# A hybrid decoder layer: z's blocks by sevens of products, and part of the state-space work on ScalarE

## The chip, the cores and the metric

The kernel runs on one core of one Trainium2 chip. The time is device microseconds of one execution. Three executions of the kernel before took 1457.78 to 1458.51 us, with a median of 1458.33. A separate execution was taken by the hardware profiler; it took 1458.42 us, of which its trace spans 1456.6. Engines are called by the profile's names: PE (TensorE), PEld (its weight loads), DVE (VectorE), ACT (ScalarE), POOL (GpSimd), SP (SyncE).

## What is computed

One layer for 256 tokens of width 2048, all in float32. The part that matters is the first half, `hybrid_mixer`, cut:

```python
u = rmsnorm(h)                                  # (256, 2048)
z, xbc, dt_raw, q, k, v = split(u @ w_in)       # z: 2048 columns; x: 2048, B and C: 1024 each; dt: 32; q, k, v: 2048 each
xs, bm, cm = split(silu(causal_depthwise_conv(xbc, conv_w, conv_b)))     # four taps
dt = softplus(dt_raw + dt_bias)                 # 32 heads in 8 groups of 4
a_cs = cumsum(dt * -exp(a_log))                 # inside chunks of 128 tokens
decay_in = exp(where(causal, a_cs[i] - a_cs[j], -inf))
y = (C B^T * decay_in) (x dt) + C state * exp(a_cs) + d_skip * x
y_ssm = groupnorm(y * silu(z)) * ssm_norm_w
y_att = dilated_window_attention(q, k, v)
h = h + rmsnorm(concat(y_ssm, y_att) @ w_out)
h = h + rmsnorm(relu(rmsnorm(h) @ w_up)^2 @ w_down)
```

## The kernel before

**Products in three parts.** A float32 operand is split in two: `hi` is its value rounded to PE's format (ACT, L147) and `lo` what is left (a subtraction on DVE, L148). A product is then three matmuls: hi by hi, hi by lo, lo by hi. Weights come in tiles of 256 rows by 512 columns, loaded by SP as `raw` (128 partitions x 1024), split into `hi` and `lo`, and used. One index `k` stands for 256 inputs, so eight of them make up the 2048. There are a few buffers for each, and PE's progress frees them.

**Plain work and sevens.** In plain work by tokens (`row_tile`, L328 to L330) two halves of the tokens, two halves of `k` and three matmuls make 12 matmuls of 128x512 for a block of 512 columns, so 24 for two blocks. A *seven* (`seven`, L411 to L413) takes two blocks at once and replaces the eight products of two token halves, two input halves and two blocks by seven products of sums (21 matmuls). Before it, sums of the activations are formed once for a `k` (`sums_of_acts`, L368 to L371 and a split), and for each seven sums of the weights (`add_in_line`, L252) that are split as well. `combine_new` (L420 to L424) puts the extra accumulators together. A `unit` runs a list of such `k` for two blocks, some plain and some by seven, and ends with plain ones. It takes all eight accumulator banks.

**Pairs.** For a seven, the sum of two weight tiles (a *pair*) comes from DRAM: POOL loads one tile to a place in DRAM (L276) and adds the other to it with a second, accumulating transfer (L277); SP loads the result later. `plan` lists the pairs in order, and `next_pair` issues the next. There are five places, and the first use of each is preceded by a tiny transfer (L275) that waits for a certain tile. In the kernel before, sevens are used from the second block of keys on, and the first four pairs are issued there.

**The state-space stage** (about the first 360 us). For each half: a block of B, one of C, then twice a block of x and one of z. B, C and x are computed with features on partitions (`gemm_features`, L473 and L476), put together (`added`, L496 and L497), scaled, and run through the convolution (`conv`: a padded copy on L736, the first tap on L741, three more on L743, and SiLU on L745). z is computed by tokens (`gate_block`, with SiLU on L751). In between, generators in a queue, `waiting`, are advanced a step at each `pump()`: `steps` (dt: a product on L660 and L661 with weights `raw_dt`, which ACT's queue loads on L653, then a chain of small DVE operations up to L693 and the cumulative sums on L698 to L706), and `ssd_group`, one for each of the eight groups (decay exponents on L790, their exponential on L791, the state products on L795 and after). `rstd` (1 / root mean square of each token) is made by POOL on L142.

**Order.** Each engine carries out its instructions in the order of its queue. A scheduler sets that order from the program's; work under `high_priority` goes ahead of other work.

**After the mixer**, `mix_to_up` adds the output product to h, normalizes it, and turns its rows by blocks of 128 (`turn`, L1108) to be the operand of the next product. `turn(t, n)` turns the four blocks of token half t and column block n.

Of the kernel before, what the change touches and what calls it, by code (L numbers as in the profile page):

```python
# [77 lines left out]
def hymba_layer(ctx: ExitStack, tc: tile.TileContext, x, norm_mix_pre, w_in, conv_w, conv_b, dt_bias, a_log,  # L78
# [177 lines left out]
    w_v, w_ups, w_downs = w_in[:, COL_V:], [w_up[:, hf * 4096:] for hf in range(2)], [w_down, w_down[4096:]]  # L256
# [10 lines left out]
    def next_pair():  # L267
# [6 lines left out]
        if len(paired) < len(places):  # L274
            nc.gpsimd.dma_start(d[:, 0:1], sh[:, NK - 1, 0:1].bitcast(F32))  # L275
# [149 lines left out]

    for n in (0, 2):
        plan("v", w_v, n, range(7), V_SEVENS)
# [223 lines left out]
    def steps():  # L651
# [16 lines left out]
        y = sp1.tile([P, NT, 32], F32, name="dt_y")  # L668
        for t in range(NT):
            nc.vector.scalar_tensor_tensor(y[:, t], p[:, t * 32:(t + 1) * 32], rstd[:, t:t + 1], bias_b,  # L670
                                           op0=ALU.mult, op1=ALU.add)

        e = sp1.tile([P, NT, 32], F32, name="dt_e")
        nc.vector.scalar_tensor_tensor(e, y, -1.0, y, op0=ALU.mult, op1=ALU.min)
        nc.scalar.activation(e, e, AF.Exp)
        r = sp1.tile([P, NT, 32], F32, name="dt_r")
        nc.vector.tensor_scalar(r, e, 2.0, None, op0=ALU.add)
        nc.vector.reciprocal(r, r)
        s = sp1.tile([P, NT, 32], F32, name="dt_s")
        nc.vector.tensor_mul(s, e, r)  # L680
        q = sp1.tile([P, NT, 32], F32, name="dt_q")
        nc.vector.tensor_mul(q, s, s)
        h = sp1.tile([P, NT, 32], F32, name="dt_h")
        nc.vector.tensor_scalar(h, q, 2.0 / 17, None, op0=ALU.mult)
        for n in (15, 13, 11, 9, 7, 5, 3):
            nc.vector.scalar_tensor_tensor(h, h, 2.0 / n, q, op0=ALU.add, op1=ALU.mult)
        nc.vector.scalar_tensor_tensor(h, h, 2.0, s, op0=ALU.add, op1=ALU.mult)
        nc.vector.scalar_tensor_tensor(dt, y, 0.0, h, op0=ALU.max, op1=ALU.add)
        ea = sp1.tile([P, 32], F32, name="dt_a")
        nc.scalar.activation(ea, a_b, AF.Exp)  # L690
# [41 lines left out]
    def conv(dst, ft0):  # L732
        for b in range(2):
# [4 lines left out]
            for f in range(2):  # L738
                ft = ft0 + 2 * b + f
                d = dst[:, 2 * b + f]  # L740
                nc.vector.tensor_scalar(d, pad[:, f, 3:], cw[:, 3, ft:ft + 1], None, op0=ALU.mult)  # L741
# [5 lines left out]
    def gate_block(c0):  # L747
        acc = gemm_tokens(w_in, c0, act_u, NK)
        dst = mp.tile([P, NT, NB], F32, name="tk", bufs=3)
        for t in range(NT):  # L750
            nc.scalar.activation(dst[:, t], acc[t], AF.Silu, scale=rstd[:, t:t + 1])  # L751
        return dst

    def ssd_group(sp, g, bT, cT, xT, z):
# [3 lines left out]
        nc.scalar.dma_start(bc, acs_d[hs].partition_broadcast(P))  # L758

# [9 lines left out]
        nc.vector.tensor_copy(bn, p[:, S:S + P])  # L769
# [16 lines left out]
        for c in range(NT):  # L786
            m = bc[:, :, c * P:(c + 1) * P]
            for r in range(HPG):
                h = HPG * g + r
                nc.vector.tensor_scalar(m[:, r], m[:, r], acs[:, c, h:h + 1], 0.0, op0=ALU.subtract, op1=ALU.min)  # L790
            nc.scalar.activation(m, m, AF.Exp)  # L791
            nc.vector.tensor_tensor(m, m, cbm[:, c, None, :].to_broadcast([P, HPG, P]), op=ALU.mult)
# [4 lines left out]
        nc.vector.tensor_copy(st, p[:, :S])  # L797
# [34 lines left out]
    sp = ssd.enter_context(tc.tile_pool(name="sp", bufs=2, side="right", reuse_waits="tile"))  # L832
    for hb in range(2):
# [644 lines left out]
```

## Time and profile before

| | |
|---|---|
| median of three runs | 1458.33 us (1457.78 to 1458.51) |
| profiled execution | 1458.42 us |
| its span | 1456.6 us |
| mean granted PE clock | 0.999 |
| instructions in the trace | 20308 |
| matmuls | 7117 |
| moved by DMA | 325.10 MB |

Rows of the trace give a start, a duration, the engine, the line, the operation with `out<-in`, sizes, a count, and in brackets how long the engine was idle before it and what released it. Rows of groups give count, busy time, mean ns of one, and the idle time before. A line number is one of the kernel before. Matmuls overlap on PE: one that lasts 0.39 us is followed by the next in less, so that starts are to be compared, not durations. ACTq is ACT's queue issuing a DMA.

### The profile page before, as it was taken

What the parts mean: (1) busy time and instruction counts of PE and PEld (TensorE: products, weight loads), DVE (VectorE), ACT (ScalarE), POOL (GpSimd) and SP (SyncE); (2) the same over time, 40 slices, a digit from 0 to 9 for tenths busy, and PEclk for the clock granted to TensorE, in tenths of its full rate; (3) what the DMA queues carried; (4) which work ended last, traced back from release to release, by engine and by line L of the source; (5) the groups of instructions that cost most, each with busy time, mean ns of one, the idle gap of its engine ahead of it and who ended that gap; (6) DMA issues with size and microseconds to landing.
All of it is one profiled execution on the core that took longest, in us unless ns stands there. A gap on an engine that the chain in (4) does not pass through costs nothing.

```text
span 1456.6 us, 20308 instructions
## 1 busy us (share of the span) xinstructions
PE 1448.5 (99%) x7117; PEld 1222.2 (84%) x7117; DVE 1268.3 (87%) x1886; ACT 897.8 (62%) x1227; POOL 146.2 (10%) x214
## 2 busy tenths in 40 slices
PE   9999999999999999999999999999999999999998
PEld 8888888888888888888888888888888888888886
DVE  6798897798987686689878999999889999999997
ACT  7465665465666556556557577666454776766663
POOL 0003100211110000001100111011111111101000
PEclk9999999999999999999999999999999999999999
DMA  8766666567875486688876798678888888798854
GB/s 270 209 205 179 184 179 197 178 175 231 237 224 174 130 235 209 191 255 270 260 226 216 205 313 242 193 227 253 241 248 279 251 245 245 210 293 263 250 176 159
DMA packets 168758, 325.10 MB, mean 223 GB/s; under 512 B 15328, under 2 KB 18256, under 8 KB 168656
## 3 DMA queue, kind: packets, MB, share of 16 engines
q1 hardware_dynamic: 144496, 272.37, 58.3%
q0 software_dynamic: 16288, 37.76, 13.2%
q10 hardware_dynamic: 7872, 13.68, 2.7%
q8 instruction: 56, 0.92, 0.2%
q14 instruction: 46, 0.38, 0.1%
HBM read 319.53 MB, written 41.98 MB: 248 GB/s over the span
## 4 chain that ended last, share of the span: by engine, by line
PE 99%; DVE 0%; ACT 0%; issue 0%; ACTq 0%
PE acc L473 15%; PE acc L328 12%; PE acc L330 12%; PE acc L329 12%; PE acc L476 8%; PE acc L413 6%; PE acc L411 6%; PE acc L412 6%; PE ps L330 3%; PE ps L329 3%; PE ps L328 3%; PE ps L413 2%; PE ps L411 2%; PE ps L412 2%; PE ps L807 1%; PE acc L1385 1%
## 5 line engine op out<-in xcount | busy, mean ns | idle before, releaser
L147 ACT ACTIVATE hi<-raw 128x1024 fp32r<-128x1024 f32 (+1 forms) x392 | 409.8, 1051 | 268.6 <-PE acc L473 92.2
L148 DVE TENSOR_TENSOR lo<-raw,hi 128x1024 fp32r<-128x1024 f32 (+1 forms) x392 | 476.9, 1221 | 92.7 <-ACT hi L147 88.7
L473 PE MATMUL acc<-ua,hi 128*128 128x512 f32 x600 | 163.5, 401 | 0.0
L473 PEld LDWEIGHTS acc<-ua,hi 128*128 128x128 f32 x600 | 105.7, 189 | 16.7
L147 ACT ACTIVATE hi<-e 128x1024 fp32r<-128x1024 f32 x64 | 68.0, 1063 | 71.4 <-DVE e L252 66.3
L328 PE MATMUL acc<-hi,ua 128*128 128x512 f32 x248 | 98.4, 397 | 0.0
L330 PE MATMUL acc<-hi,ua 128*128 128x512 f32 x248 | 96.8, 390 | 0.0
L476 PEld LDWEIGHTS acc<-ua,lo 128*128 128x128 f32 x600 | 88.2, 189 | 10.3
L329 PE MATMUL acc<-lo,ua 128*128 128x512 f32 x248 | 96.7, 390 | 0.0
L476 PE MATMUL acc<-ua,lo 128*128 128x256 f32 x600 | 90.8, 281 | 0.0
L328 PE MATMUL acc<-hi,sh 128*128 128x512 f32 x224 | 88.4, 395 | 0.0
L330 PE MATMUL acc<-hi,sl 128*128 128x512 f32 x224 | 87.3, 390 | 0.0
L329 PE MATMUL acc<-lo,sh 128*128 128x512 f32 x224 | 87.2, 389 | 0.0
L148 DVE TENSOR_TENSOR lo<-e,hi 128x1024 fp32r<-128x1024 f32 x64 | 77.9, 1218 | 0.0
L473 PE MATMUL acc<-uc,hi 128*128 128x512 f32 x240 | 68.5, 397 | 0.0
L411 PE MATMUL acc<-hi,ah 128*128 128x512 f32 x174 | 67.8, 389 | 0.0
L412 PE MATMUL acc<-lo,ah 128*128 128x512 f32 x174 | 67.7, 389 | 0.0
L413 PE MATMUL acc<-hi,al 128*128 128x512 f32 x174 | 67.7, 389 | 0.0
L148 DVE TENSOR_TENSOR lo<-ha,hi 128x1024 fp32r<-128x1024 f32 x43 | 52.4, 1220 | 6.0 <-ACT hi L147 5.7
L147 ACT ACTIVATE hi<-ha 128x1024 fp32r<-128x1024 f32 x43 | 45.3, 1057 | 18.3 <-PE acc L330 9.8
L330 PEld LDWEIGHTS acc<-hi,ua 128*128 128x128 f32 x248 | 46.6, 188 | 10.0
L328 PEld LDWEIGHTS acc<-hi,ua 128*128 128x128 f32 x248 | 46.6, 188 | 9.4 <-ACT ua L149 0.3
(543 smaller groups left out, 3510.9 us busy)
## 6 DMA issues: line engine op xcount, KB each, us to landing
raw<-in_w_in_dram SPq DMA_DIRECT2D x167, 512.0 KB, 3.9
raw<-in_w_down_dram SPq DMA_DIRECT2D x72, 512.0 KB, 5.2
raw<-in_w_up_dram SPq DMA_DIRECT2D x65, 512.0 KB, 4.6
raw<-in_w_out_dram SPq DMA_DIRECT2D x38, 512.0 KB, 5.0
pair<-in_w_up_dram POOLq DMA_DIRECT2D x56, 256.0 KB, 5.3
pair<-in_w_down_dram POOLq DMA_DIRECT2D x50, 256.0 KB, 6.3
raw<-pair SPq DMA_DIRECT2D x46, 256.0 KB, 4.6
ha<-in_w_up_dram SPq DMA_DIRECT2D x20, 512.0 KB, 5.7
```

Source lines behind the costliest of these rows:

```text
L147: return (nc.scalar.activation(hi, src, AF.Copy), nc.vector.tensor_tensor(lo, src, hi.bitcast(F32), op=ALU.subtract))
L148: nc.vector.tensor_tensor(lo, src, hi.bitcast(F32), op=ALU.subtract))
L328: nc.tensor.matmul(dst, a_h[:, r, ts], hi[:, j], start=begin and j == 0, stop=False)
L329: nc.tensor.matmul(dst, a_h[:, r, ts], lo[:, j], start=False, stop=False)
L330: product[t] = nc.tensor.matmul(dst, a_l[:, r, ts], hi[:, j], start=False, stop=end and j == KB - 1)
L411: nc.tensor.matmul(dst, a_h, hi[:, j], start=own and first, stop=False)
L412: nc.tensor.matmul(dst, a_h, lo[:, j], start=False, stop=False)
L413: nc.tensor.matmul(dst, a_l, hi[:, j], start=False, stop=own and last)
L473: nc.tensor.matmul(acc[f], hi[:, j, f * P:(f + 1) * P], u(k0 + j), start=k0 + j == 0, stop=False, skip_group_check=True)
L476: nc.tensor.matmul(acc[f][:, 0], lo[:, j, f * P:(f + 1) * P], u(k0 + j)[:, 0], start=False, stop=k0 + j == NK - 1, skip_group_check=True)
L807: nc.tensor.matmul(p[:, c, r], bc[:, r, c * P:(c + 1) * P], xdt[:, c, r], start=True, stop=True)
L1385: nc.tensor.transpose(p[:, f * P:(f + 1) * P], r[:, f * P:(f + 1) * P], ident)
```

## The change

1. **z by sevens.** The four calls of `gate_block` become two calls of `gates`, after the first and the third block of x. Each is a `unit` of two blocks, with `k` in the orders (0, 2, 4, 6, 1, 3, 5) and (0, 2, 1, 4, 3, 6, 5), sevens for 1, 3 and 5, and 7 plain at the end.
2. **Pairs from the start.** z's six pairs are listed ahead of the others. The first four are issued as soon as `u(15)`, the last tile of u, is there.
3. **Sums of activations** for k = 1, 3, 5 are made in the first stage, and once more for the keys.
4. **To ScalarE:** the first tap of the convolution, the exponents of decay (four activations Relu for each chunk of 128, with -1 as scale and the cumulative sum as bias, then the exponential with scale -1), and the copies `bn` and `st`.
5. **Order:** the dt chain goes ahead of other work and its products come some steps later in the count of steps; a group waits a step after its DMA; the first keys advance the queue two steps and one in turn instead of one; and in `mix_to_up` `turn(0, 2)` comes ahead of `turn(1, 0)`, with the banks set by a list.

```diff
-    w_v, w_ups, w_downs = w_in[:, COL_V:], ...
+    w_z, w_v, w_ups, w_downs = w_in[:, COL_Z:], w_in[:, COL_V:], ...
...
-            nc.gpsimd.dma_start(d[:, 0:1], sh[:, NK - 1, 0:1].bitcast(F32))
+            nc.gpsimd.dma_start(d[:, 0:1], u(NK - 1)[:, 0, 0:1].bitcast(F32))
...
+    plan("z", w_z, 0, (0, 2, 4, 6, 1, 3, 5), (1, 3, 5))
+    plan("z", w_z, 2, (0, 2, 1, 4, 3, 6, 5), (1, 3, 5))
...
         yield
-        for t in range(NT):
-            nc.vector.scalar_tensor_tensor(dA[:, t], dt[:, t], -1.0, ea, op0=ALU.mult, op1=ALU.mult)
-        yield
-        yield
+        with tc.high_priority(offset=AHEAD):
+            for t in range(NT):
+                nc.vector.scalar_tensor_tensor(dA[:, t], dt[:, t], -1.0, ea, op0=ALU.mult, op1=ALU.mult)
+        for _ in range(7):
+            yield
...
-                nc.vector.tensor_scalar(d, pad[:, f, 3:], cw[:, 3, ft:ft + 1], None, op0=ALU.mult)
+                nc.scalar.activation(d, pad[:, f, 3:], AF.Copy, scale=cw[:, 3, ft:ft + 1])
...
-    def gate_block(c0):
-        acc = gemm_tokens(w_in, c0, act_u, NK)
-        dst = mp.tile([P, NT, NB], F32, name="tk", bufs=3)
-        for t in range(NT):
-            nc.scalar.activation(dst[:, t], acc[t], AF.Silu, scale=rstd[:, t:t + 1])
-        return dst
+    def gates(n):
+
+        room["own"] = deque(mp.tile([P, NT, NB], F32, name="tk", bufs=3)[:, t] for t in range(NT))
+        place_of_sums()
+        room["sums"] = [v[:, k:k + KB] for k in range(NK // 2, NK, KB) for v in (sh, sl)]
+        room["raw"], room["turn"], room["acts"] = [], 0, act_u
+        gated = [mp.tile([P, NT, NB], F32, name="tk", bufs=3) for _ in range(2)]
+
+        def end(b):
+            def at_end(t, a):
+                with tc.high_priority(offset=AHEAD):
+                    v = gated[b][:, t]
+                    nc.vector.tensor_tensor(v, a, v, op=ALU.subtract if b else ALU.add)
+                    nc.scalar.activation(v, v, AF.Silu, scale=rstd[:, t:t + 1])
+            return at_end
+
+        unit(w_z, n, orders["z", n], (7,), *eight_banks(),
+             lambda x: combine_new([[v[:, t] for t in range(NT)] for v in gated], x), 0, (end(0), end(1)))
+        return gated
...
         nc.scalar.dma_start(bc, acs_d[hs].partition_broadcast(P))
+        yield
...
-        nc.vector.tensor_copy(bn, p[:, S:S + P])
+        nc.scalar.activation(bn, p[:, S:S + P], AF.Copy)
...
-                nc.vector.tensor_scalar(m[:, r], m[:, r], acs[:, c, h:h + 1], 0.0, op0=ALU.subtract, op1=ALU.min)
-            nc.scalar.activation(m, m, AF.Exp)
+                nc.scalar.activation(m[:, r], m[:, r], AF.Relu, scale=-1.0, bias=acs[:, c, h:h + 1])
+            nc.scalar.activation(m, m, AF.Exp, scale=-1.0)
...
-        nc.vector.tensor_copy(st, p[:, :S])
+        nc.scalar.activation(st, p[:, :S], AF.Copy)
...
+    with tc.high_priority(offset=AHEAD):
+        for _ in range(PAIRS_AHEAD):
+            next_pair()
+    zs = []
...
-            z = gate_block(COL_Z + xb * NB)
+            if xb % 2 == 0:
+                zs += gates(xb)
...
-    qk = [keys_too(0)]
+    qk = [keys_too(0, (2, 1))]
...
+    sums_of.clear()
...
-    with tc.high_priority(offset=AHEAD):
-        for _ in range(PAIRS_AHEAD):
-            next_pair()
...
-            turn(1, 0)
-            turn(0, 2)
+            turn(0, 2)
+            turn(1, 0)
```

Three queues show what this does to the order. The first is POOL's at the program's start; before, it held memsets of the convolution's edges (`pad`), then `rstd`, then more memsets:

```order
L735 MEMSET pad 128x2x3 x2
L142 ISA
L142 TENSOR_TENSOR rstd<-rm,half 128x2
L735 MEMSET pad 128x2x3 x6
L781 TENSOR_TENSOR xdd<-xdt,toend 128x256
```

After the change the five tiny transfers (L275) and then these rows stand there:

```order
L276 DMA pair_89<-in_w_in_dram 128x512
L276 DMA pair_90<-in_w_in_dram 128x512
L276 DMA pair_91<-in_w_in_dram 128x512
L276 DMA pair_92<-in_w_in_dram 128x512
L277 DMA pair_89<-in_w_in_dram 128x512
L277 DMA pair_90<-in_w_in_dram 128x512
L277 DMA pair_91<-in_w_in_dram 128x512
L277 DMA pair_92<-in_w_in_dram 128x512
L276 DMA pair_93<-in_w_in_dram 128x512
L739 MEMSET pad 128x2x3 x2
L142 ISA
L142 TENSOR_TENSOR rstd<-rm,half 128x2
```

So nine transfers of z's weights have moved ahead of the first memsets and of `rstd`.

The second is DVE's queue while PE works on the first z block. Before, subtractions for the weights (`lo`) alternate with the convolution of x (L736 to L743):

```order
L148 TENSOR_TENSOR lo<-raw,hi 128x1024
L743 SCALAR_TENSOR_TENSOR cT<-pad,cw,cT 128x256 x2
L736 TENSOR_TENSOR pad<-cT,rbc 128x2x256
L743 SCALAR_TENSOR_TENSOR cT<-pad,cw,cT 128x256
L741 TENSOR_SCALAR cT<-pad,cw 128x256 x2
L148 TENSOR_TENSOR lo<-raw,hi 128x1024
L743 SCALAR_TENSOR_TENSOR cT<-pad,cw,cT 128x256 x4
L148 TENSOR_TENSOR lo<-raw,hi 128x1024
```

After the change this is the second of the first unit's sevens (its first two additions stand just ahead) and the third:

```order
L148 TENSOR_TENSOR lo<-raw,hi 128x1024
L252 TENSOR_TENSOR tk<-cT,raw 128x512
L148 TENSOR_TENSOR lo<-cT,hi 128x1024
L148 TENSOR_TENSOR lo<-raw,hi 128x1024
L148 TENSOR_TENSOR lo<-tk,hi 128x512
L252 TENSOR_TENSOR cT<-raw 128x512
L252 TENSOR_TENSOR cT<-cT,raw 128x512
L148 TENSOR_TENSOR lo<-raw,hi 128x1024
L252 TENSOR_TENSOR tk<-cT,raw 128x512
L148 TENSOR_TENSOR lo<-cT,hi 128x1024
L148 TENSOR_TENSOR lo<-raw,hi 128x1024
L148 TENSOR_TENSOR lo<-tk,hi 128x512
```

Each seven now stands there as three additions of weights and four subtractions, without other work between the last two of them.

The third is ACT's queue where the first two groups' decays are made (`bc`). Before, this was behind the first z block, and ACT made only the exponentials (L791):

```order
L147 ACTIVATE hi<-raw 128x1024
L776 ACTIVATE xs<-ps 128x512
L791 ACTIVATE bc<-bc 128x4x128
L147 ACTIVATE hi<-raw 128x1024
L791 ACTIVATE bc<-bc 128x4x128 x2
L776 ACTIVATE xs<-ps 128x512
```

After the change the exponents (L816) and the exponentials (L817) stand among the splits of the first unit's sevens:

```order
L147 ACTIVATE hi<-raw 128x1024
L816 ACTIVATE bc<-bc,acs 128x128
L147 ACTIVATE hi<-tk 128x512
L147 ACTIVATE hi<-raw 128x1024
L816 ACTIVATE bc<-bc,acs 128x128 x3
L817 ACTIVATE bc<-bc 128x4x128
L816 ACTIVATE bc<-bc,acs 128x128 x4
L147 ACTIVATE hi<-cT 128x1024
L147 ACTIVATE hi<-raw 128x1024
L147 ACTIVATE hi<-tk 128x512
L420 ACTIVATE tk<-ps 128x512
```

So eight of the small activations and one exponential are now in the same queue between two splits of weights.

More of the change, by code (lines that the diff above doesn't have):

```diff
@@ L1066, in mix_to_up @@
         up = [bank() for _ in range(NT)]
[L1067 removed]
+        banks, turned = {}, {}
+        turns = [(0, 0), (0, 1), (1, 0), (0, 2), (1, 1), (1, 2), (1, 3), (0, 3)]
         weighed = hp.tile([P, NT, NB], F32, name="e")
```

67 lines of the change are left out of this document (34 added, 33 removed).

## Prediction, before the result was known

> **What bounds the kernel now.** I read the page's busy shares and its chain first, then the busy time by stretches of 40 us, then single stretches of the trace. The page says who sets the end:
>
> ```profile
> span 1456.6 us, 20308 instructions
> PE 1448.5 (99%) x7117; PEld 1222.2 (84%) x7117; DVE 1268.3 (87%) x1886; ACT 897.8 (62%) x1227; POOL 146.2 (10%) x214
> PE 99%; DVE 0%; ACT 0%; issue 0%; ACTq 0%
> ```
>
> The chain that ended last is TensorE almost from end to end. Whether that holds in the stages that the change touches (0 to 360 us) is in the stretches; the columns are the stretch, PE, weight load, DVE, ACT, POOL, clock, DMA share and GB/s:
>
> ```profile
> 0.00:40.00 40.00, 38.94 (x224) 34.70 (x225) 25.32 (x43) 27.06 (x55) 1.13 (x7) 1.00 0.83 267
> 40.00:80.00 40.00, 40.00 (x245) 35.68 (x244) 31.94 (x60) 22.18 (x29) 0.21 (x2) 1.00 0.67 201
> 80.00:120.00 40.00, 40.00 (x209) 33.84 (x208) 38.92 (x88) 27.46 (x39) 7.20 (x10) 1.00 0.64 197
> ...
> 280.00:320.00 40.00, 40.00 (x210) 34.04 (x209) 38.76 (x80) 28.40 (x41) 7.72 (x8) 1.00 0.63 182
> ...
> 360.00:400.00 40.00, 40.00 (x179) 33.16 (x178) 39.22 (x53) 23.85 (x28) 7.11 (x11) 1.00 0.90 246
> ```
>
> PE is busy all of the time, and DVE, at 38.92 of 40 where z0 stands, is close behind. So a product that PE need not do is time gained, and there is no idle PE time there to win besides. What counts is whether DVE, ACT and the DMAs still arrive first. Busy time hides overlap, so the price of a product is read from starts:
>
> ```profile
> 82.19 0.40 PE L328 MATMUL acc<-hi,ua 128*128 128x512 f32 x1
> 82.42 0.40 PE L329 MATMUL acc<-lo,ua 128*128 128x512 f32 x1
> ...
> 90.83 0.39 PE L330 MATMUL acc<-hi,ua 128*128 128x512 f32 x1
> ```
>
> From 82.19 to 90.83 there are 38 steps: (90.83 - 82.19) / 38 = 0.227 us a product, though one lasts 0.39.
>
> **The sum, against 1458.42 us** for the profiled execution (span 1456.6 and 1.8 around it); the median of the three runs is 1458.33, so the same differences are taken from the median.
>
> *Products.* Two units of two z blocks have three sevens each, and a seven has 21 products where plain work has 24: 6 x 3 = 18 fewer, 18 x 0.227 = **-4.1 us**. The small products between them stay the same in kind.
>
> *Transposes.* PE waits once here:
>
> ```profile
> 771.03 0.74 DVE L1099 SCALAR_TENSOR_TENSOR ha<-mw,rmix,ha 128x512 f32<-128x512 f32 x1
> 772.22 0.75 DVE L1099 SCALAR_TENSOR_TENSOR ha<-mw,rmix,ha 128x512 f32<-128x512 f32 x1
> 773.03 0.65 PE L1108 MATMUL acc<-ident,ha 128*128 128x128 f32 x4 [0.23 <-DVE ha L1099]
> ```
>
> `turn(1, 0)` needs the row of 772.22, ready at 772.97; `turn(0, 2)` needs the earlier one, of 771.77. With their order turned the wait of 0.23 goes, **-0.2** (0 to -0.4); what is late next is `turn(1, 0)`, which now comes one group of four transposes later, when its row is there.
>
> *DVE's and ACT's load.* The prices, as mean ns after the busy sum, by groups of equal shape:
>
> ```profile
> L148 DVE TENSOR_TENSOR lo<-raw,hi 128x1024 fp32r<-128x1024 f32 x113 | 141.1, 1250 | 32.1 <-ACT hi L147 30.9 <-PE acc L476 0.3
> L147 ACT ACTIVATE hi<-raw 128x1024 fp32r<-128x1024 f32 x113 | 119.2, 1057 | 116.2 <-PE acc L473 72.8 <-PE acc L330 19.1 <-issue 15.3
> L148 DVE TENSOR_TENSOR lo<-tk,hi 128x512 fp32r<-128x512 f32 x12 | 8.2, 684 | 0.0
> L252 DVE TENSOR_TENSOR cT<-raw 128x512 f32<-128x512 f32 x7 | 4.8, 686 | 0.9 <-DMA raw<-pair 0.9
> L790 DVE TENSOR_SCALAR bc<-bc,acs 128x128 f32<-128x128 f32 x64 | 13.9, 282 | 0.0
> L741 DVE TENSOR_SCALAR cT<-pad,cw 128x256 f32<-128x256 f32 x32 | 10.0, 347 | 0.0
> L864 ACT ACTIVATE sm<-sm,mx 128x128 f32<-128x128 f32 x16 | 6.3, 397 | 7.1 <-DVE mx L862 7.1
> L864 ACT ACTIVATE sm<-sm,mx 128x256 f32<-128x256 f32 x16 | 8.0, 497 | 1.9 <-DVE mx L862 1.9
> ```
>
> A seven costs DVE 3 additions, 3 subtractions of 128x1024 and one of 128x512: 3 x 0.69 + 3 x 1.25 + 0.68 = 6.5 us, while PE needs 21 x 0.227 = 4.8. A plain step costs DVE 2 x 1.25 = 2.5 and PE 24 x 0.227 = 5.4. Over the stage DVE gains 6 x (6.5 - 2.5) = 24 for the sevens, 16 x 0.68 = 11 for combining them, and at most 15 x 0.69 = 10 for three sums of activations; it loses 64 x 0.28 = 18, 32 x 0.35 = 11 and the copies: +16 at most in 360 us. ACT gets 64 x 0.40 = 26 and 32 x 0.50 = 16, in all some 50 busy us. That is less in wall time, since neighbours overlap by about 0.1, and it fits: before its 113 splits ACT now waits 116 us, 92 of them for PE to free a buffer, so it is ahead of PE.
>
> The tight place is z0, where three sevens follow each other (k = 1, 3, 5). How far is DVE ahead?
>
> ```profile
> 74.21 1.23 DVE L148 TENSOR_TENSOR lo<-raw,hi 128x1024 fp32r<-128x1024 f32 x1
> ```
>
> This is the subtraction for z0's first tile, done at 75.4; PE takes it up at 82.42 (above): 7.0 us. Three sevens use up 3 x (6.5 - 4.8) = 5.1, which leaves about 2. The conv operations that went to ACT add a little, sums and X0's conv inside the sevens take it again. I put **+0.2** (0 to 0.7). z2's order alternates plain and seven, 2.5 + 6.5 against 5.4 + 4.8, so it costs nothing. Three small places are left: where z ends, a subtraction for X1's weights stands behind one that waits for z's last accumulators; `st`, now copied on ACT, can stand behind a split; and the first block gets two sums. Without any lead they would cost what they stand behind, about 0.7, 1.06 and twice 0.69; with a lead like the one above, nothing. I take **+0.3** together, near the covered end (0 to 1).
>
> *The dt chain and POOL's queue.* The cumulative sums of decay stood inside z0 and now end X0, some 10 us earlier:
>
> ```profile
> 91.19 0.63 PE L698 MATMUL ps<-dA,cst 128*128 128x32 f32 x4
> ```
>
> Their chain on DVE goes ahead of other work now and ends beside z0's first subtraction, so near 75, while PE comes there just before 82.19: **0**. If that cover were gone, PE would wait the difference. On POOL, refills of pairs now stand ahead of memsets and of `xdd` and wait for a seven's load; in z0 that is over before PE reaches the groups' state products, which its order has behind z0: **0**.
>
> *DMAs at the start.* The pairs were primed at 353 us. Now they start once `u(15)` is written, near 29 us, ahead of POOL's memsets and `rstd`:
>
> ```profile
> 353.08 2.92 POOL L275 DMA_DIRECT2D pair<-sh  x5 [15.59 <-ACT sh L149]
> 358.93 2.23 POOL L276 DMA_DIRECT2D pair<-in_w_in_dram  x4 [2.93 <-DMA pair<-sh]
> ...
> 368.53 1.03 POOL L276 DMA_DIRECT2D pair<-in_w_in_dram  x1
> 378.02 0.81 POOL L277 DMA_DIRECT2D pair<-in_w_in_dram  x1 [8.46 <-DMA pair<-in_w_in_dram]
> ```
>
> From the first to the last of those ahead of `rstd` it took 16.5 us, so `rstd` would come at 29 + 16.5 = 45.5 or so instead of 38.78. Its first reader does not run before 47.79, so this is **0**:
>
> ```profile
> 38.78 0.72 POOL L142 TENSOR_TENSOR rstd<-rm,half 128x2 f32<-128x2 f32 x1 [2.45 <-DVE rm L141]
> 47.79 0.28 DVE L632 TENSOR_SCALAR dg<-ident,rstd 128x128 f32<-128x128 f32 x1
> ```
>
> But the transfers land in the busiest stretch for the DMA engines:
>
> ```profile
> 38.00:40.00 2.00, 2.00 (x12) 1.67 (x11) 0.66 (x4) 0.10 (x1) 0.72 (x1) 1.00 1.16 300
> 36.04 0.39 ACTq L653 DMA_DIRECT2D raw_dt<-in_w_in_dram  x1
> 45.04 0.63 ACT L147 ACTIVATE wdt<-raw_dt 128x512 fp32r<-128x512 f32 x1 [2.65 <-DMA raw_dt<-in_w_in_dram]
> 45.70 0.69 DVE L148 TENSOR_TENSOR wdt<-raw_dt,wdt 128x512 fp32r<-128x512 f32 x1 [2.05 <-ACT wdt L147]
> 49.27 0.28 PE L660 MATMUL ps<-ua,wdt 128*64 128x256 f32 x1
> ```
>
> `raw_dt` takes 45.04 - 36.04 = 9.0 us beside the weights' queue alone; its tile is ready at 46.39, 2.9 us before PE wants it. With a third queue in equal turns it would take 9.0 x 3/2 = 13.5, and L660 would start 1.6 late; by the priming of before it costs 0, since PE was busy 40.00 of 40 beside it at a DMA share of 0.90. If the weight tiles behind suffer too, 3. I take **+0.4**, a quarter of 1.6, as the priming is the same nine transfers and so the nearer row. The Trainium skill (DMA: Bandwidth & Descriptors, section "Queues, rings and completion order") says that each DMA engine goes round the queues that have work, a packet of each in turn: that is the case of 1.6, and by it the sum would be 1.2 us higher; the rows of `raw_dt` alone cannot tell.
>
> Sum: -4.1 - 0.2 + 0.2 + 0.3 + 0.4 = **-3.4**: 1455.0 for a profiled run like this one, **1454.9** from the median.
>
> **The rivals.** *No stall at all*: -4.3, 1454.0, and 1453.8 with the transposes' other end. For it: PE's 40.00 in every stretch. Against: four new places where something may come late.
>
> *The start's transfers bite*: 1.6 to 3 us at L660 instead of 0.4, so 1456.1 to 1457.5. For it the DMA share of 1.16 at 38 us; against it the priming of before.
>
> *DVE is not ahead in z0*: if the lead of 7.0 is gone by the first seven, all 5.1 us are lost, 4.9 more than in the sum: 1459.8. For it, DVE's 38.92 of 40 there; against it, the lead just measured.
>
> *Slower: ACT's new work stands before the splits.* Each of 16 chunks of decays now has four 128x128 activations on ACT before its exponential. At 0.40 less the overlap that is some 1.4 us during which no split starts, and the queue is in order. If half of the chunks find no lead, 8 x 1.4 = 11 are lost: 1458.3 - 4.3 + 11 = 1465. It decides from (4.3 + 2.9) / 1.4 = 5 exposed chunks on. For it: two groups' chunks now lie among z0's sevens, which want 3 x 1.06 + 0.63 = 3.8 us of ACT in 4.8. Against it: the 92 us that ACT waits for PE. The Trainium skill (ScalarE: Activation LUTs, section "Rules for kernel authors") says that relu, add and the like belong on VectorE and not on ScalarE. The rows agree engine for engine, 0.28 against 0.40; by that rule alone the move would be a loss.
>
> *The change does not do what it says*: 18 products fewer stand in the order of its instructions, so I give this nothing.
>
> **How the numbers follow.** A difference of 0.2%, 2.9 us, is about what a measurement can tell from no change: faster is under 1455.4, slower over 1461.2. The forecast has 0.53, its own range 1454.2 to 1455.8, of which 0.05 lies within 0.2%. No stall 0.10 (faster). Start's transfers 0.13 and DVE in z0 0.12 (within 0.2%, bar 0.01 of the latter where both meet). ACT 0.12 (slower). So faster 0.48 + 0.10 = 0.58, same 0.05 + 0.13 + 0.11 = 0.29, slower 0.13. The range reaches from 1453.8 to 1459.9, over all but ACT's rival and a little of the others, some 0.85.
>
> **What would show it.** In the new trace: 18 products of 128x512 fewer and PE without idle from 40 to 360; L660's counterpart near 49.3, or late with `raw_dt` as what it waited for; in z0's third seven no wait on a subtraction; the transposes' 0.23 gone. Idle PE time in front of products whose weights were split on ACT behind decays would make the forecast wrong, and so would more than 1 us at L660.

## The result, and the profile after

The changed kernel takes 1470.00 us, the median of six runs (1467.68 to 1471.31), against 1458.33 for the kernel before: a ratio of 1.0079 (95% interval 1.0069 to 1.0090). The forecast was 1454.9, and its range ended at 1459.9. The profiled execution took 1471.31 us (before: 1458.42), so it has to account for 12.9 us.

The page of the kernel after: its head and its chain.

```profile
span 1469.3 us, 20379 instructions
PE 1450.1 (99%) x7099; PEld 1223.3 (83%) x7099; DVE 1277.6 (87%) x1835; ACT 938.4 (64%) x1352; POOL 149.7 (10%) x226
PE 84%; DVE 1%; ACT 0%; issue 0%; POOL 0%; DVEq 0%; ACTq 0%
```

The 18 products are gone (7117 to 7099). That the chain is TensorE for 84% only, where it was 99%, is no measure of idle time: the chain leads back only to 207.5 us, where it leaves TensorE for DVE, and what lies before is not in it. PE is busy for 1450.1 of the 1469.3 us. The table of waits for PE's engine says what it waited for (us in total, times, longest), and the stretches of 40 us say where and at which clock (the columns are those of the prediction):

```profile
PE ps L662 <- DVE wdt L148: 7.1, 1, 7.1
PE ps L821 <- DVE sl L150: 2.6, 1, 2.6
...
PE acc L556 <- DMA xs<-in_x_dram: 0.6, 1, 0.6
PE ps L789 <- ACT bn L795: 0.5, 1, 0.5
PE ps L833 <- DVE yo L827: 0.3, 1, 0.3
PE acc L329 <- DVE lo L148: 0.2, 1, 0.2
PE ps L412 <- DVE lo L148: 0.2, 1, 0.2
```

```profile
40.00:80.00 40.00, 32.91 (x187) 29.45 (x186) 21.05 (x43) 16.42 (x22) 4.93 (x9) 0.91 0.78 218
...
200.00:240.00 40.00, 37.35 (x218) 32.89 (x217) 32.81 (x60) 29.26 (x59) 3.25 (x8) 0.96 0.56 171
```

Two waits are new and long: one at the product for dt (L662 is the L660 of before), one at a group's state product (L821, before L795). Both stretches also show a lower clock. The two lines left out are waits that the kernel before has too.

**The first wait.** Rows of the timeline of the kernel after, on POOL, ACT and PE:

```profile
30.44 2.89 POOL L275 DMA_DIRECT2D pair<-uc  x5 [29.99 <-ACT uc L149]
...
37.47 0.39 ACTq L655 DMA_DIRECT2D raw_dt<-in_w_in_dram  x1
56.56 0.63 ACT L147 ACTIVATE wdt<-raw_dt 128x512 fp32r<-128x512 f32 x1 [9.16 <-DMA raw_dt<-in_w_in_dram]
57.10 3.88 ACT L147 ACTIVATE hi<-raw 128x1024 fp32r<-128x1024 f32 x4
57.97 0.47 PE L662 MATMUL ps<-ua,wdt 128*64 128x256 f32 x1 [7.09 <-DVE wdt L148]
```

`raw_dt` is 56.56 - 37.47 = 19.1 us on its way (9.0 before), and L662 starts at 57.97 (49.27 before). ACT stands idle for 9.16 us ahead of `wdt`, and four splits of weights that stand behind it in ACT's queue run one after another as soon as it is through. The DMA view of 28 to 60 us, of the kernel after (packets, MB, share of 16 engines' time; issues with KB and median us to landing):

```profile
q1 hardware_dynamic: 2566, 4.93, 45.0%
q0 software_dynamic: 1280, 2.62, 37.7%
q10 hardware_dynamic: 2064, 0.26, 5.3%
...
raw_dt<-in_w_in_dram ACTq DMA_DIRECT2D x1, 256.0 KB, 19.1
```

and the same of the kernel before:

```profile
q1 hardware_dynamic: 3651, 7.05, 71.9%
q10 hardware_dynamic: 2064, 0.26, 5.3%
```

q10 carries `raw_dt`: 0.26 MB in 2064 packets, so about 128 bytes each, while q1 (the weights) moves some 1.9 KB a packet and q0 (the pairs) 2.0 KB. My reading is that a load of that many small packets takes many turns among the queues, and that each turn now has a packet of q0 in it; the part on the prediction weighs this. In the sixteen runs of this case without the early pairs `raw_dt` takes 6.0 to 9.6 us, in the three with them (after, e3, e4) 18.7 to 19.7.

**The clock behind it.** Stretches of 1 us of the kernel after, behind each of the two waits:

```profile
56.00:57.00 1.00, 0.00 (x0) 0.00 (x0) 0.00 (x0) 0.44 (x1) 0.00 (x0) 0.54 0.84 122
58.00:59.00 1.00, 1.00 (x5) 1.00 (x6) 0.83 (x1) 1.00 (x3) 0.00 (x0) 0.50 0.00 0
62.00:63.00 1.00, 1.00 (x7) 1.00 (x6) 1.00 (x2) 0.00 (x0) 0.00 (x0) 0.55 0.96 330
63.00:64.00 1.00, 1.00 (x11) 1.00 (x10) 0.26 (x1) 0.00 (x0) 0.00 (x0) 1.00 0.99 350
...
209.00:210.00 1.00, 1.00 (x6) 0.91 (x5) 0.84 (x2) 0.56 (x2) 0.00 (x0) 0.84 0.97 358
210.00:211.00 1.00, 1.00 (x4) 0.71 (x4) 1.00 (x2) 0.00 (x0) 0.00 (x0) 0.50 0.79 291
213.00:214.00 1.00, 1.00 (x8) 0.84 (x6) 0.00 (x0) 0.49 (x2) 0.00 (x0) 0.95 0.88 332
```

PE is granted half its clock from about 56.1 to 62.9 us, 6.8 in all; it works from 57.97 on, so some 4.9 us at half speed, 2.4 lost. Behind the second wait it is half from 209.7 to 213.1: 3.4 us, 1.7 lost.

**The second wait.** The state product (L821) waits for a bank of `ps` that `sl` has yet to read. DVE in the kernel after, up to that product:

```profile
201.63 3.25 DVE L747 SCALAR_TENSOR_TENSOR cT<-pad,cw,cT 128x256 f32<-128x256 f32 x8
204.80 0.47 DVE L150 SCALAR_TENSOR_TENSOR sl<-ps,par,sh 128x256 fp32r<-128x256 f32 x1
205.20 2.34 DVE L148 TENSOR_TENSOR lo<-raw,hi 128x1024 fp32r<-128x1024 f32 x2
...
207.86 0.86 DVE L150 SCALAR_TENSOR_TENSOR sl<-ps,par,sh 128x256 fp32r<-128x256 f32 x2
208.47 0.67 PE L821 MATMUL ps<-xdd,bn 128*128 128x256 f32 x2 [2.65 <-DVE sl L150]
```

DVE has no gap here, from 190 us on: the convolution of the second half's C block, splits of weights and the ends of groups follow each other. In the 10 us before, from 180 to 190 us, it is busy for 6.38 us only, and 1.9 us of the rest are waits for splits on ACT, which is busy for 9.94. So DVE comes late to its crowd, and ACT has a part in that.

Added up at the first product of the keys (360.42 us before, 373.28 after, +12.9): the waits 7.1 + 2.65, the two halved clocks 2.4 + 1.7, the first block 1.4 (C0's first product is at 33.88 us in place of 32.43 in this execution, xs's 0.6 is part of it; over all profiled executions of this case it lies between 31.9 and 34.8, with and without the change), the short waits 0.5 + 0.3 + 0.2, less the products' 4.1. That is 12.2 of 12.9. (Of the two waits of 0.2 for `lo`, the one at L412 is at 126.53 us; the one at L329 is at 787.01, long behind the keys' first product.) From that point to the end the two kernels take 1096.2 and 1096.0 us.

### The profile page after: what moved, and what is told of

Same layout as the page of the kernel before. It is cut to its first block, busy times and chain, and to the rows that moved or that the text cites. A ratio compares the mean times of both kernels' runs of the same rounds, so it can differ in the third digit from the quotient of the medians.

```text
span 1469.3 us, 20379 instructions
## 1 busy us (share of the span) xinstructions
PE 1450.1 (99%) x7099; PEld 1223.3 (83%) x7099; DVE 1277.6 (87%) x1835; ACT 938.4 (64%) x1352; POOL 149.7 (10%) x226
## 4 chain that ended last, share of the span: by engine, by line
PE 84%; DVE 1%; ACT 0%; issue 0%; POOL 0%; DVEq 0%; ACTq 0%
PE acc L330 11%; PE acc L329 11%; PE acc L328 11%; PE acc L475 9%; PE acc L411 6%; PE acc L413 6%; PE acc L412 6%; PE acc L478 5%; PE ps L328 3%; PE ps L330 3%; PE ps L329 3%; PE ps L411 2%; PE ps L413 2%; PE ps L412 2%; PE ps L833 1%; PE acc L1408 1%
## 5 line engine op out<-in xcount | busy, mean ns | idle before, releaser
L329 PE MATMUL acc<-lo,sh 128*128 128x512 f32 x224 | 87.2, 389 | 0.0
L328 PE MATMUL acc<-hi,ua 128*128 128x512 f32 x216 | 85.5, 396 | 0.0
L329 PE MATMUL acc<-lo,ua 128*128 128x512 f32 x216 | 84.3, 390 | 0.2 <-DVE lo L148 0.2
L330 PE MATMUL acc<-hi,ua 128*128 128x512 f32 x216 | 84.3, 390 | 0.0
L412 PE MATMUL acc<-lo,ah 128*128 128x512 f32 x174 | 67.8, 389 | 0.0
L413 PE MATMUL acc<-hi,al 128*128 128x512 f32 x174 | 67.7, 389 | 0.0
L147 ACT ACTIVATE hi<-r 128x512 fp32r<-128x512 f32 x64 | 40.2, 627 | 18.2 <-PE acc L330 7.1
L330 PE MATMUL acc<-hi,al 128*128 128x512 f32 x128 | 49.8, 389 | 0.0
```

The costliest lines, as they stand in the source:

```text
L147: return (nc.scalar.activation(hi, src, AF.Copy), nc.vector.tensor_tensor(lo, src, hi.bitcast(F32), op=ALU.subtract))
L328: nc.tensor.matmul(dst, a_h[:, r, ts], hi[:, j], start=begin and j == 0, stop=False)
L329: nc.tensor.matmul(dst, a_h[:, r, ts], lo[:, j], start=False, stop=False)
L330: product[t] = nc.tensor.matmul(dst, a_l[:, r, ts], hi[:, j], start=False, stop=end and j == KB - 1)
L412: nc.tensor.matmul(dst, a_h, lo[:, j], start=False, stop=False)
L413: nc.tensor.matmul(dst, a_l, hi[:, j], start=False, stop=own and last)
```

## Experiments

Four theories stood at the outset. A: the pairs' transfers hold up `raw_dt`, and the loss at the first wait follows from it. B: `raw_dt` is late for another reason, such as the first block's new sums. C: the second wait is only an order of ready work on DVE. D: ACT's new work makes DVE late. Two more came from the first runs. E: DVE has too little time in the state-space stage once sevens are in it, whatever its order. F: where the groups' steps stand decides. Each run is measured beside runs of the kernel before (1458.34 to 1458.64 in these comparisons).

### e1_pairs_after_dt: the pairs start behind the dt columns

```diff
-            nc.gpsimd.dma_start(d[:, 0:1], u(NK - 1)[:, 0, 0:1].bitcast(F32))
+            nc.gpsimd.dma_start(d[:, 0:1], room["gate"].bitcast(F32))
...
         split(wdt[:, :, 0:32], wdt[:, :, 32:64], raw)
+        room["gate"] = wdt[:, 0, 0:1]
+        for _ in range(PAIRS_AHEAD):
+            next_pair()
...
-    with tc.high_priority(offset=AHEAD):
-        for _ in range(PAIRS_AHEAD):
-            next_pair()
```

> The changed kernel, but the first pairs wait for the split of raw_dt (wdt) instead of u(15), and stand behind rstd on POOL. Theory A (the nine transfers of pairs share the DMA engines with raw_dt and the weights): raw_dt lands some 9 us after its issue as in the kernel before, the idle of 7.1 us at L662 and the half clock behind it (2.4 us) go, about 1460.5; the 2.65 us at the state product (L821) stay. Theory B (raw_dt is late for another reason, such as the first block's new sums or the weight loads): 1468 or more, and raw_dt still takes some 19 us.

1460.43 us (1458.34 to 1462.70), ratio 1.0012 (1.0003 to 1.0021). Rows of its timeline:

```profile
42.53 0.63 ACT L147 ACTIVATE wdt<-raw_dt 128x512 fp32r<-128x512 f32 x1 [1.13 <-DMA raw_dt<-in_w_in_dram]
43.49 2.92 POOL L275 DMA_DIRECT2D pair<-wdt  x5 [4.20 <-ACT wdt L147]
```

`raw_dt` takes 6.7 us (9.0 in the kernel before), the pairs start at 43.49, PE waits for nothing there, and 9.6 of the 11.7 us are back. The profiled execution took 1459.02 us, 1.4 less than the median, so its trace need not show all that e1 still loses.

### e3_before_pairs_first: the kernel before, with only the early pairs

```diff
-            nc.gpsimd.dma_start(d[:, 0:1], sh[:, NK - 1, 0:1].bitcast(F32))
+            nc.gpsimd.dma_start(d[:, 0:1], u(NK - 1)[:, 0, 0:1].bitcast(F32))
...
     sp = ssd.enter_context(tc.tile_pool(name="sp", bufs=2, side="right", reuse_waits="tile"))
+    with tc.high_priority(offset=AHEAD):
+        for _ in range(PAIRS_AHEAD):
+            next_pair()
...
     waiting.append(sums_ahead())
-    with tc.high_priority(offset=AHEAD):
-        for _ in range(PAIRS_AHEAD):
-            next_pair()
```

> The kernel before, with only one thing changed: its first four pairs (v's) are issued when u(15) is there, not at 353 us. No sevens for z, nothing moved to ACT. Theory A: L660 waits some 7 us and the clock halves behind it, 1458.3 + 9.5 = about 1468. Theory B: no wait, 1458.3 to 1459.

1468.87 us (1467.98 to 1469.90), ratio 1.0070 (1.0055 to 1.0085). Its waits for PE, and its stretch with the clock:

```profile
PE ps L660 <- DVE wdt L148: 6.7, 1, 6.7
```

```profile
40.00:80.00 40.00, 33.29 (x193) 29.61 (x192) 22.28 (x41) 15.47 (x20) 5.78 (x10) 0.91 0.80 224
```

Taken out, the early pairs give 9.6 us back; put alone into the kernel before, they cost 10.5. A is shown from both sides, with the clock's part in it, and B falls.

### e4_sl_ahead, e14_both: the wait's own operation put first

```diff
-            split(sh[:, k], sl[:, k], p[:, f], w_ssm[:, k:k + 1])
+            with tc.high_priority(offset=AHEAD):
+                split(sh[:, k], sl[:, k], p[:, f], w_ssm[:, k:k + 1])
```

> The changed kernel, with the split of the finished state-space rows (sh, sl) put ahead of the convolution's work. Theory C (the state product L821 waits for a bank that sl has not yet read, because sl stands behind twelve operations of the convolution on DVE): the idle of 2.65 us there and the half clock behind it (about 2 us) go, 1470.0 - 4.6 = 1465.4. Rival (DVE as a whole is late there by the sevens and the first taps that come from ACT): the wait moves to another product and the time stays within 1 us of 1470.

1471.20 us (1470.28 to 1472.23), ratio 1.0086 (1.0071 to 1.0101). The wait for `sl` is gone and another output of DVE is late in its place:

```profile
PE ps L662 <- DVE wdt L148: 7.7, 1, 7.7
PE ps L833 <- DVE yo L827: 2.2, 2, 2.0
```

> Both of these edits in the changed kernel. If A and C hold and add up: 1470.0 - 9.5 - 4.6 = about 1456, less than the kernel before; if one of them only moves the wait, 1460 or more.

e14_both is that edit on e1's kernel: 1465.03 us (1461.51 to 1466.37), ratio 1.0033 (1.0019 to 1.0048), worse than e1 although its wait is shorter. The stretches of 4 us say why: in the profiled execution (1465.65 us) the clock is halved for 0.3 + 4 + 4 + 1.9 = 10.2 us, which costs 5.1. The other executions fit: the two near 1461.7 us have a mean granted clock of 0.997 and 0.998, the two above 1465 of 0.994 and 0.996.

```profile
198.00:202.00 4.00, 2.02 (x14) 1.70 (x13) 2.89 (x5) 2.31 (x3) 0.83 (x2) 0.96 0.58 139
202.00:206.00 4.00, 4.00 (x18) 3.83 (x18) 1.24 (x2) 0.00 (x0) 0.00 (x0) 0.50 0.49 186
...
210.00:214.00 4.00, 4.00 (x20) 3.37 (x19) 1.30 (x3) 1.82 (x6) 0.00 (x0) 0.76 0.43 131
```

C falls: to put this operation ahead of other ready work only moves the wait.

### e5_decays_on_dve, e7_all_on_dve, e14_acts_alone: the moves to ScalarE

e5 is e1 with the decays' exponents back on DVE; e7 has the first tap and the two copies back as well. e14_acts_alone is the kernel before with these moves and nothing else of the change (and is not the e14 of e12's expectation, which is e14_both).

```diff
-                nc.scalar.activation(m[:, r], m[:, r], AF.Relu, scale=-1.0, bias=acs[:, c, h:h + 1])
-            nc.scalar.activation(m, m, AF.Exp, scale=-1.0)
+                nc.vector.tensor_scalar(m[:, r], m[:, r], acs[:, c, h:h + 1], 0.0, op0=ALU.subtract, op1=ALU.min)
+            nc.scalar.activation(m, m, AF.Exp)
```

> As e1_pairs_after_dt (pairs behind dt, 1460.4 us), with the decays' exponents back on DVE; first tap and copies stay on ACT. Theory D (ACT is what makes DVE late ahead of the state product: DVE waits some 3 us for ACT between 170 and 181): the wait of 2.6 us at the state product shrinks, about 1456 to 1458. Theory E (DVE itself has more work than time around C1's convolution, so that what ACT took was a help): the wait grows or others come, 1461 to 1464.

> As e1_pairs_after_dt, with the decays' exponents, the first tap and both copies back on DVE, so that of the change the sevens, the pairs and the order are left. Theory D: 1456 to 1458. Theory E: DVE gets 29 us of work back in the stage, more waits in front of products split on DVE, 1462 or more.

> The kernel before with only the moves to ScalarE (decays' exponents, the convolutions' first tap, the copies bn and st); z's blocks, the pairs, the dt columns and the transposes as before. If VectorE is short of time only when the products of seven add to its load: TensorE waits for nothing between 80 and 400 us before, so there is nothing to win, and the time stays within 1 us of 1458.4. If the moves to ScalarE cost something by themselves: a wait for bn or cT on ScalarE of 0.5 us or more, and 1459.0 to 1461.

e5: 1461.15 us (1460.08 to 1462.70), ratio 1.0018 (1.0008 to 1.0028). e7: 1463.87 (1463.31 to 1464.56), ratio 1.0037 (1.0024 to 1.0050). e14_acts_alone: 1458.32 (1457.79 to 1460.00), ratio 0.9998 (0.9989 to 1.0007). Waits of e7:

```profile
PE ps L824 <- DVE sl L150: 2.9, 2, 1.5
PE ps L329 <- DVE lo L148: 1.5, 1, 1.5
```

As a remedy D falls: with the exponents back on DVE the time is not shorter (e5), and with all of the moves taken back it is 1463.87 - 1460.43 = 3.4 us longer (e7). But ACT has a part in this one wait, as D says: at this product it is 2.64 us in e1, 1.69 in e5 and 1.50 in e7. What is won there comes back as a wait at the same product in the second half, 1.84 us at 334.85 in e5 and 1.40 at 332.01 in e7. Part of e7's loss lies behind the stage: its 1.5 us for `lo` is at 406.84, among the keys, and from the keys' first product on e7 takes 1098.9 us where e1 takes 1096.1. E stands in this form: beside sevens the moves to ACT help DVE; without sevens, where PE waits for nothing between 80 and 400 us, they win and cost nothing.

### e8_no_step_more, e9_step_before_state: the places of the groups' steps

e8 is e1 without the `yield` that the change put behind the DMA of `bc`; e9 is e1 with one more, ahead of the state product.

> As e1_pairs_after_dt, without the step that each group now waits after its DMA. Theory F (the wait comes from where the groups' steps fall: state products of two groups beside C1's convolution and beside the turning of two groups before): the wait changes its place and size, and the time moves by more than 1 us either way. If the load of DVE or ACT as such decides (D or E): within 1 us of 1460.4, with the same wait elsewhere.

> As e1_pairs_after_dt, with one step more in each group, ahead of its state product, so that C1's convolution is done on DVE by then. Theory F: the 2.6 us and what the clock loses behind it go, 1455 to 1457. D or E: DVE's lateness comes out at another product, 1459 or more.

e8: 1458.76 us (1457.84 to 1460.28), ratio 1.0004 (0.9995 to 1.0013). e9: 1463.71 (1463.02 to 1463.88), ratio 1.0035 (1.0022 to 1.0048). Waits of e8, then of e9:

```profile
PE ps L835 <- DVE yo L829: 1.1, 1, 1.1
PE ps L855 <- DVE yg L848: 0.9, 2, 0.7
```

```profile
PE acc L411 <- ACT hi L147: 3.5, 3, 2.2
```

One step less is worth 1.7 us by the medians, though the two intervals overlap, and one more costs 3.3. For e9 the expectation by F was 1455 to 1457, which was missed, but its trace shows that F holds in the stage itself. The wait of 2.6 us is gone, with 1.0 at 336.01 us left, and e9 comes to the keys' first product at 358.80, earlier than the kernel before (360.42) and e1 (360.28). It loses at the keys: the waits shown above and 1.5 us for `lo` lie between 373 and 407 us, the longest of them here:

```profile
379.16 0.50 PE L411 MATMUL acc<-hi,ah 128*128 128x512 f32 x1 [2.17 <-ACT hi L147]
```

From the keys' first product to the end e9 takes 1103.1 us, the kernel before 1096.2. The groups' last transposes now stand at 358.44, right ahead of the keys (351.02 in e1), and ACT waits there for sums from DVE. That DVE is late with the keys' sums because the groups' work ends later is argued from this order; no run that has e9's step and makes room at the keys tests it. F stands beside E: a step's place decides what a group's work collides with, and that can lie behind the stage.

### e10_ahead_two, e11_ahead_three, e12_ahead_all_in_e1, e13_z0_alternate: order once more

e10 puts `yo` and the normalising of `yg` ahead on DVE in e8, e11 the `sh`/`sl` split as well; e12 does all three in e1. e13 is e8 with the first unit's terms in the second's order.

```diff
-    plan("z", w_z, 0, (0, 2, 4, 6, 1, 3, 5), (1, 3, 5))
+    plan("z", w_z, 0, (0, 2, 1, 4, 3, 6, 5), (1, 3, 5))
```

> The kernel of e8 with two short operations on VectorE put ahead of what else is ready there: yo (L829 there) and the normalising of yg (L848 there). In e8's profiled run they are waited for 1.1 us (product L835) and 0.9 us (transposes L855). If only their order among ready work is at fault, both waits go, nothing takes their place, and the time falls by about 2.0 us to some 1456.7. If VectorE is short of time over this stretch whatever its order, another VectorE output is waited for by TensorE for 1 to 4 us, and the time stays at 1458 to 1460 or rises.

> As e10, and the split into sh and sl that closes each block also goes ahead. If order alone matters: as e10, 1456.7. If VectorE is short of time: a wait for yo, for yg or for a convolution's output, and no better than e8's 1458.8.

> The kernel of e1 (the change, its pairs started behind the dt columns' split) with yo, the normalising of yg and the split into sh and sl put ahead on VectorE. e14 put the split alone ahead and the wait moved to yo (2.2 us, 1465.0). If order alone matters: no wait above 1 us between 90 and 360 us, and about 1457.0 (e1's 1459.0 profiled, less 2.6, and some of what its spread holds). If VectorE is short of time there: the wait moves once more, to xdd, bn or a convolution's output, and the time is 1459 to 1466.

> The kernel of e8 with the first z unit's seven-product and pair terms in the order that the second has (0, 2, 1, 4, 3, 6, 5 in place of 0, 2, 4, 6, 1, 3, 5), so that VectorE's additions for them are spread differently over z0. Less than 0.7 us either way if the order within the unit is covered by TensorE's products; a wait at the unit's start or end of 1 to 3 us if the sums that the terms need are formed too late in that order.

e10: 1459.19 us (1457.64 to 1462.25), ratio 1.0007 (0.9998 to 1.0016). e11: 1459.03 (1457.29 to 1460.15), 1.0002 (0.9993 to 1.0011). e12: 1461.49 (1460.92 to 1464.75), 1.0025 (1.0016 to 1.0034). e13: 1459.12 (1458.50 to 1462.49), 1.0008 (0.9999 to 1.0017). Nothing is won: `yo` is still waited for 1.1 us in e10 and e11, 2.2 in e12, and e13 has `xdd` (made by POOL) 0.7 and `cT` (by ACT) 0.6 in its place. But e8 and e10 show the clock side by side. Both wait 1.1 us near 145 us; a stretch of 2 us behind it in e8, and three in e10:

```profile
148.00:150.00 2.00, 2.00 (x17) 1.90 (x16) 1.60 (x3) 1.42 (x3) 0.00 (x0) 1.00 0.81 292
```

```profile
146.00:148.00 2.00, 2.00 (x18) 1.96 (x17) 0.55 (x1) 0.17 (x1) 0.16 (x1) 0.93 0.78 203
148.00:150.00 2.00, 2.00 (x10) 1.82 (x9) 0.83 (x2) 1.79 (x5) 0.00 (x0) 0.50 0.89 285
150.00:152.00 2.00, 2.00 (x16) 2.00 (x14) 0.42 (x1) 0.00 (x0) 0.72 (x1) 0.72 0.30 96
```

### e15_norm_on_act, e16_norm_on_act_alternate: less load on DVE

The normalising of `yg` goes to ScalarE, in e8's kernel and in e13's.

```diff
-            nc.vector.tensor_scalar(yg[:, c], yg[:, c], gr[:, c:c + 1], None, op0=ALU.mult)
+            nc.scalar.activation(yg[:, c], yg[:, c], AF.Copy, scale=gr[:, c:c + 1])
```

> The kernel of e8 with the normalising of yg (two 128x256 operations a group) on ScalarE in place of VectorE. If VectorE's load is what is left of the waits: those for yo (1.1 us) and yg (0.9 us) shrink to under 0.5 us together and the time is 1456.5 to 1457.3. If the places of the groups' steps decide: a wait of 1 us or more stays or moves, and the time stays at 1458 to 1459.5.

> As e15, on the kernel of e13 (the first z unit's terms alternating). In e13's profiled run the waits in the stage are yg 0.9, xdd 0.7, cT 0.6 and lo 0.5 us. If VectorE's load is what is left: yg's wait goes and the time is 1456 to 1457. If not: 1458 to 1459.5, with the waits for cT and xdd as they were or longer, since ScalarE has more to do.

e15: 1459.20 us (1457.04 to 1462.90), ratio 1.0004 (0.9995 to 1.0013). e16: 1458.91 (1458.01 to 1461.46), 1.0004 (0.9995 to 1.0013). In e15 the waits shrink to 0.7 (`yo`) and 0.6 (`yg`), a split's `hi` is waited for 0.6 instead, and the time stays. Two operations a group less on DVE change nothing that these times can tell.

### e17_last_two_sevens, e18_last_two_sevens_step: only the second unit

z's first two blocks are as before, the last two a unit with three sevens. The pairs' DMAs were meant to come behind the second block; they went forward to 46.8 us, but stayed behind `wdt`.

```diff
-            if xb % 2 == 0:
-                zs += gates(xb)
+            if hb == 0:
+                zs.append(gate_block(COL_Z + xb * NB))
+            elif xb == 2:
+                zs += gates(2)
```

> The kernel of e8 with z's first two blocks as in the kernel before and only its last two as a unit with three groups of seven; the first four pairs start behind the second of those blocks. Half of the products' gain is left, 9 products of 0.227 us: 2.0 us. If VectorE is crowded between 130 and 230 us because of the first unit (its sums, and two blocks' groups that then fall due together), no output of VectorE is waited for there, and the time is 1456.3 to 1457.0. If the last unit's own work, or the moves to ScalarE, are what keeps TensorE waiting, a wait of 0.7 us or more shows between 230 and 360 us and the time is 1457.5 to 1459.

> As e17, with the change's extra step at the head of each group. If the step's place is of no account where VectorE isn't crowded: as e17 within 0.5 us. If it decides: a wait of 1 us or more that e17 lacks, and 1 to 3 us more.

e17: 1457.36 us, ratio 0.9990 (0.9981 to 0.9999); one of its eleven executions took 2959.70 us, which nothing here explains, the others 1457.05 to 1459.14. e18: 1457.63 (1457.06 to 1458.81), ratio 0.9994 (0.9985 to 1.0003). Of e17, stretches and waits:

```profile
80.00:160.00 80.00, 80.00 (x425) 68.48 (x424) 62.26 (x102) 65.21 (x121) 10.40 (x16) 1.00 0.64 192
160.00:240.00 80.00, 80.00 (x471) 70.58 (x471) 64.94 (x103) 62.08 (x110) 11.29 (x16) 1.00 0.64 186
```

```profile
PE ps L859 <- DVE yg L852: 0.7, 1, 0.7
```

Without the first unit PE waits for nothing from 80 to 240 us in e17, and in e18 only 0.6 us, for a copy on ACT (`bn`). So the waits for DVE there come with the first unit: its sevens, and the groups of two blocks of x, which fall due together behind it. Which of the two weighs more was not taken apart. Neither time of the expectation was met: 1457.36 lies between the two, and the wait of 0.7 us that the second one named is there as well, at 345.44. The extra step, worth 1.7 us in e1 against e8, is worth 0.3 here. e17 is the only version that beats the kernel before by more than its interval, by 1.3 us, and barely so: the interval ends at 0.9999, and it is the best of seventeen runs. Of its 2.0 us of products 0.7 go to `yg`'s wait.

## Why the prediction was wrong, step by step

**The step that failed is the term for DMAs at the start**: +0.4, with bounds of 0 and 3, where the trace has 7.1 + 2.4 = 9.5 us, e1 gives 9.6 and e3 10.5. The wait and its place (L660, for `raw_dt`) were named; three things in its pricing were wrong. First, the size of a turn. I took three queues as turns of equal length, 9.0 x 3/2 = 13.5 us. The DMA view gives lengths: as share x 16 engines x 32 us / packets, a packet of q0 takes 0.377 x 512 / 1280 = 0.151 us, one of q1 0.090 (0.101 before), one of q10 0.013. By those a round grows from 0.114 to 0.254, an estimate of 2.2 times; `raw_dt` grew 19.1 / 9.0 = 2.1 times. So close a fit is in part luck: 6.0 to 9.6 us without the early pairs make it 2.0 to 3.2 times. Nor do the rounds come out one by one, since 2048 packets on 16 engines are 128 rounds, 14.6 and 32.5 us by these prices where 9.0 and 19.1 were measured. The rule that was weighed and discounted there (the Trainium skill, DMA: Bandwidth & Descriptors, section "Queues, rings and completion order": the engines go round the queues packet by packet) agrees with the ratio; whether its packets are those that the profile counts, no run here shows. That the early pairs hold up `raw_dt` is shown by e1 and e3; that they do so by the length of their packets is argued, as no run changes that length. Second, the nearer row was not near: the priming at 353 us cost nothing, and no load of 128-byte packets was on its way beside it: of the kernel before, the DMA view of 350 to 380 us has data on q1 and q0 only.

```profile
q1 hardware_dynamic: 3269, 6.28, 60.5%
q0 software_dynamic: 1140, 2.37, 35.8%
```

Third, the price of the wait ended at L662: the half clock behind the stop, another 2.4 us, was left out. The four splits that were held up behind `wdt` on ACT cost PE no wait of their own in the list.

**Missing altogether: the second wait.** I followed DVE's lead in z0 alone. It held there (one wait of 0.2 us for `lo`, at 126.53, as the +0.2 said), so the rival of 1459.8 did not come; the crowd came some 80 us later, in the C block, 2.65 us and 1.7 of clock. The sum of DVE's load over 360 us (+16 at most) could not show it, since the stretch's mean is not what is waited for.

**Right:** the products (7099, and e17, which does half of them and wins 1.3 of 2.0); `rstd` (at 44.71, its 45.5 forecast) and the dt chain, both unseen by PE. Of the three small places one showed under another name: `bn`, a copy moved to ACT, 0.5 us.

**Also wrong, by 0.2: the transposes.** Their wait (L1108 before, L1131 after) is gone as forecast, but the second product behind the turned blocks now waits 0.25 us for `lo` (L329, at 787.01). From the stage's first group of transposes to its fifth it takes 9.48 us before (765.96 to 775.44) and 9.48 after (778.81 to 788.29), so the term is 0 and not -0.2.

**The slower rival did not come about.** PE waits for no `hi` in the stage, and e14_acts_alone prices all moves at 0. In a weak form its mechanism is there: between 180 and 190 us DVE waits 1.9 us for splits on a full ACT, and the second wait is 1.0 us shorter without the exponents on ACT (e5). The rule that speaks for it (the Trainium skill, ScalarE: Activation LUTs, section "Rules for kernel authors": relu and the like on VectorE) holds for one operation's price, 0.28 against 0.40; beside sevens all the moves together are nevertheless worth 3.4 us in e7 against e1, where the waits grow at DVE's outputs.

**Open:** with the start mended, e1 and e8 reach the keys about as early as the kernel before (360.28 and 360.59 against 360.42), and their new waits up to there, 3.3 and 2.8 us in all, leave 0.7 and 1.4 us of the products' 4.1 that no row names. Nor does e1's trace, one of its shorter executions, show what makes its median 2.1 us longer than that of the kernel before.

## What to carry to other kernels

Before new transfers are started early, look for a load of many small packets on another queue, and do not price it by the number of queues alone: the DMA view's packet times gave a better guess here, with the reservations above. A gate on the tile that this load makes left PE without a wait there. Products taken from a busy TensorE are won only where the engine that feeds it delivers in time in that very stretch, and behind it. A busy share doesn't tell this: DVE is busy for 9.75, 9.91 and 9.84 of 10 us from 190 to 220 us in the kernel before, where PE waits for nothing, and for 10.00 and 9.84 from 190 to 210 after, where PE waits 2.65. Follow the lead of each output up to the product that needs it. And count each stop of TensorE with the clock that may follow it.

## What the runs showed of the hardware

TensorE's clock was halved behind stops of 1.1 us and more, and for set lengths: 3.4 us (after, behind 2.65 us), 6.8 (after, from 56.1 us on, within the stop of 7.1 and behind it), 10.2 (e14_both, behind 2.0), 3.4 (e10: 0.3 + 2 + 1.1, behind 1.1), so one, two and three times 3.4. But not behind every such stop: behind the same 1.1 us in e8, behind 2.0 in e12 (e14_both's wait) and behind 2.6 us in e1's profiled execution, it was not halved at all. e1's ten times lie near 1458.7, 1460.5 and 1462.7, as if an execution had none, one or two such lengths at 1.7 us each. The clocks on record do not bear that out: the executions of 1458.34 and of 1462.70 us both have a mean granted clock of 0.998. The kernel before, which has no such stop there, has a second level too, with five of the 21 executions measured beside e17 at 1460.45 to 1460.70 us and the others at 1457.98 to 1458.93. So the cause of these levels stays open. The Trainium skill (TensorE: Matmul & The Clock Gate, section "What's actually happening") gives a free-running window of about 3.4 us, with half rate after an idle window: the length agrees, but here a stop of a third of it was followed by half rate, so that no gap need be as long as a window.
